# Expert product of a PEER layer: one 512-column matmul for both parts of the tokens under the high weight part

## The chip, the cores and the metric

The kernel runs on one core of a Trainium2 chip. The metric is the device time in microseconds (us) of one execution, the median over several runs. The engines of the core are named as in the profile: PE does matmuls (PEld is the loading of its stationary operand), DVE, ACT and POOL are the vector, scalar and general engines, SP issues transfers. Eight banks of accumulators in PSUM stand between PE and the engines that read its results; everything else lies in SBUF.

## The reference

256 tokens of width 2048 pass through a gMLP block, a stick-breaking attention block, a block that mixes a short convolution with an mLSTM, and a PEER layer. Only the last one matters here:

```python
def peer_ffn(h, wq, keys, u, v):      # 8 heads, 16384 experts, top 16 per head and token
    q = (xt @ wq).reshape(-1, PEER_HEADS, 2, PEER_HALF)
    s = jnp.einsum('thpc,hpnc->thpn', q, keys)
    sv, si = lax.top_k(s, PEER_TOPK)                 # 16 best of 128 keys, twice per head
    ...                                              # 16 best of the 256 pairs: eid, softmax gate
    ue = jnp.take(u, eid, axis=0)
    act = jax.nn.gelu(jnp.einsum('thkd,td->thk', ue, xt), approximate=False)
    ve = jnp.take(v, eid, axis=0)
    return jnp.einsum('thk,thkd->td', gate * act, ve)
```

## The kernel before

**No gathering.** The kernel multiplies all 16384 rows of `u` with all tokens, applies Gelu, multiplies with a dense 16384 x 256 gate matrix that is zero but for the chosen experts, and multiplies the result with all of `v`. So the PEER layer is two large products: the first expert product over `in_pu` (the table `u`, stage A below) and the second over `in_pv` (accumulator `y`).

**Two parts of a number.** Matmuls take fp32r operands. To keep fp32 accuracy each operand is split into a high part (rounded to fp32r) and a low part (the rest), and a product is three matmuls: high x high, low weight x high token, high weight x low token. For the weights the class `Stream` (L87) does the split as the tables arrive: SP loads a raw tile of 128x2048 (1 MB, three buffers), ACT copies each half of it to `wh` (L123, shown as L194, since ACT's operations all go through one helper; six buffers), DVE subtracts to get `wl` (L131, five buffers). Both buffers are reused when PE has finished the half that held them. `ahead` (L139) issues these steps as far ahead as the buffers reach, so that in DVE's queue the subtraction for a half stands four halves ahead of that half's matmuls. For the tokens the split is done once, in `affine_prep` (L784), into two tiles `nh` (high) and `nl` (low).

**The first expert product** (loop L1269 over `u` in 0..31, 512 experts each) calls `gemm_t` (L381) once per `u`. Its table tile holds, per raw tile, 4 slices of 128 of the contraction (2048 = 16 slices) for all 512 experts. One half of a raw tile is 2 slices x 4 blocks of 128 experts. The experts' block is the stationary operand, the 256 tokens are the moving one. Each of the 8 (slice, block) cells of a half takes three matmuls of 256 columns, L395 (high x high), L397 (high weight, low token), L398 (low weight, high token), all added in PSUM in the same 256 columns: 24 matmuls per half, 192 per `u`. The 512 experts x 256 tokens fill two banks (`acc0`, `acc1`, two buffers each). After the last half of a `u`, ACT applies Gelu to the two banks (the lines `f<-acc`, 128x512) and SP stores the 512 KB result to DRAM (`Ad`, L1275), from where the second product loads it again.

**Background work.** Generators registered in `bg` are advanced by one yield at each `bg.step()`; `gemm_t` steps once after each half. During stage A the background holds `route` (L1143): for each of four groups of two heads (three of them in stage A, the first one mostly before it) and each of two token halves it does the key scores on PE (L411, L1156) and the two top-16 searches and the gate on DVE (L1131 to L1199), with an Exp on ACT. `scatter` (L1205) then queues the gates on POOL, one indirect transfer for each column. When nearly all `u` are done, `first_v` loads the first two stored activations and the gates, and `prep_v` (L1241) multiplies them and splits the result for the second product, one line per step.

**What sets the order.** Nothing is scheduled: each engine executes its instructions in the order in which the Python code emits them, and waits at each for the semaphores of what it needs.

Of the kernel before, what the change touches and what calls it, by code (L numbers as in the profile page):

```python
# [5 lines left out]
F32 = mybir.dt.float32  # L6
# [5 lines left out]
P = 128  # L12
D = 2048
T = 256
# [155 lines left out]
def _block(ctx, tc, A, out):  # L170
# [153 lines left out]
    def tokens(x, kk, t):  # L324

        if isinstance(x, list):
            return x[0][:, kk // 2, (2 * t + kk % 2) * P:(2 * t + kk % 2 + 1) * P]
        return x[:, kk, t * P:(t + 1) * P]
# [52 lines left out]
    def gemm_t(xh, xl, evac):  # L381


        acc = [pp.tile([P, 512], F32, name=nm("acc"), tag=f"acc{b}", bufs=2) for b in range(2)]
        for kp in range(NKT // 2):
            if kp:
                bg.step()
            wh, wl = st.next()
            for k in range(2):
                kk = kp * 2 + k  # L390
                xa, xb = (x[0][:, kp].rearrange("p (h k c) -> p k c h", h=2, k=2)[:, k] for x in (xh, xl))
                for b in range(4):
                    o = acc[b // 2][:, (b % 2) * T:(b % 2 + 1) * T].rearrange("p (c h) -> p c h", h=2)
                    c = k * 512 + b * P
                    E.matmul(o, wh[:, c:c + P], xa, start=kk == 0 and b % 2 == 0, stop=False,  # L395
                             skip_group_check=True)
                    E.matmul(o, wh[:, c:c + P], xb, start=False, stop=False, skip_group_check=True)  # L397
                    E.matmul(o, wl[:, c:c + P], xa, start=False, stop=kk == NKT - 1,  # L398
                             skip_group_check=True)
        evac(acc)  # L400
        bg.step()
# [382 lines left out]
    def affine_prep(c, d, gname, bname, paired=False):  # L784
# [3 lines left out]
        nl = tile("xs", [NKT // 2, 2 * T], F32R, bufs=4)  # L788
        if not paired:
            nh, nl = (x.rearrange("p a (k t) -> p (a k) t", k=2) for x in (nh, nl))  # L790
# [7 lines left out]
        def go(n):  # L798
            for pr in range(2):
# [18 lines left out]
                if paired:  # L818
                    hv, lv = (x[:, k // 2].rearrange("p (h k c) -> p k h c", h=2, k=2) for x in (nh, nl))
# [20 lines left out]
        return ([nh], [nl], need) if paired else (nh, nl, need)  # L840
# [279 lines left out]
    x3h, x3l, prep3 = affine_prep(*ln_scales(st6), "l1g", "l1b", True)  # L1120
# [148 lines left out]
    for u in range(NU):  # L1269
        def ev(acc, u=u):  # L1270
            a = ft(1, [2, 512])
            for b in range(2):
                act(a[:, b].rearrange("p (e h c) -> p e c h", e=2, h=2),
# [134 lines left out]
```

## Time and profile before

| | us |
|---|---|
| median of 3 runs | 3069.61 |
| lowest and highest of the 3 | 3068.31, 3072.02 |
| the profiled execution, its own time | 3071.64 |
| its span, first to last instruction | 3069.9 |

Start, end and duration of each instruction come from the profiled execution alone. Its own time is 1.7 us longer than its span. Stage A, the first expert product, goes from 1689 to 2389 us of the span, the second product from there to the end. A duration of a matmul in the trace (275 ns for 256 columns) is the time from its start to its modelled end; matmuls overlap, so what one costs is the distance from its start to the next one's start.

### The profile page before, as it was taken

How to read it: one execution, taken by the hardware profiler on the slowest of the kernel's cores; microseconds unless marked ns; L12 is line 12 of the kernel's file. 1: busy time of each engine (PE TensorE's matmuls, PEld its weight loads, DVE VectorE, ACT ScalarE, POOL GpSimd, SP SyncE). 2: the span in 40 equal slices, each digit the busy share in tenths (PEclk: the TensorE clock that was granted, in tenths of full speed). 3: DMA queues.
4: the chain of work that ended last, by engine and by line, in shares of the span. 5: the costliest groups of instructions: out<-in, count | busy, mean ns of one | idle time of the engine just before them, and what ended most of it. 6: DMA issues, size and time to landing. Idle time of an engine off the chain costs nothing.

```text
span 3069.9 us, 42972 instructions
## 1 busy us (share of the span) xinstructions
PE 3022.8 (98%) x17276; PEld 2732.7 (89%) x17276; DVE 1914.0 (62%) x2486; ACT 1502.5 (49%) x1638; POOL 553.1 (18%) x275
## 2 busy tenths in 40 slices
PE   8999999999999999999999999999999999999997
PEld 7888888888888887888888999999999888888886
DVE  6565556666555566656558989644445666666666
ACT  5454445444554555544444555544445444444443
POOL 0000000000000000000001668888883000000001
PEclk9999999999999999999999999999999999999999
DMA  7776666666555565556656777777777987888874
GB/s 275 248 248 215 218 221 224 219 213 220 197 188 200 197 233 195 206 202 208 229 187 203 208 214 210 229 222 216 227 217 262 319 274 274 283 283 285 279 256 151
DMA packets 230616, 702.55 MB, mean 229 GB/s; under 512 B 50577, under 2 KB 144913, under 8 KB 158865
## 3 DMA queue, kind: packets, MB, share of 16 engines
q1 hardware_dynamic: 192912, 697.57, 66.2%
q0 software_dynamic: 37504, 2.25, 2.8%
q8 instruction: 135, 2.21, 0.3%
q14 instruction: 65, 0.52, 0.0%
HBM read 647.18 MB, written 52.56 MB: 228 GB/s over the span
## 4 chain that ended last, share of the span: by engine, by line
PE 95%; DVE 3%; ACT 1%; DMA 1%; issue 0%; SPq 0%; DVEq 0%; ACTq 0%
PE acc L343 16%; PE acc L344 16%; PE acc L345 16%; PE acc L398 7%; PE acc L397 7%; PE acc L395 7%; PE y L345 7%; PE y L343 7%; PE y L344 7%; DVE wl L131 1%; PE ms L411 1%; PE ms L565 0%; ACT xs L194 0%; DVE res L1293 0%; PE ms L692 0%
## 5 line engine op out<-in xcount | busy, mean ns | idle before, releaser
L131 DVE TENSOR_TENSOR wl<-raw,wh 128x1024 fp32r<-128x1024 f32 x1106 | 1343.1, 1222 | 825.8 <-PE acc L344 308.9
L194 ACT ACTIVATE wh<-raw 128x1024 fp32r<-128x1024 f32 x1106 | 1166.0, 1058 | 1259.2 <-PE acc L345 578.6
L1210 POOL DMA_INDIRECT Gd<-f x256 | 536.7, 2096 | 1790.2 <-DVE f L1199 1670.1
L343 PE MATMUL acc<-wh,xs 128*128 128x512 f32 x2112 | 813.1, 385 | 14.6 <-ACT wh L194 10.1
L344 PE MATMUL acc<-wl,xs 128*128 128x512 f32 x2112 | 803.5, 380 | 0.5 <-DVE wl L131 0.5
L345 PE MATMUL acc<-wh,xs 128*128 128x512 f32 x2112 | 803.2, 380 | 0.0
L398 PE MATMUL acc<-xs,wl 128*128 128x256 f32 x2048 | 564.1, 275 | 1.6 <-DVE wl L131 1.6
L395 PE MATMUL acc<-xs,wh 128*128 128x256 f32 x2048 | 564.7, 276 | 0.0
L397 PE MATMUL acc<-xs,wh 128*128 128x256 f32 x2048 | 563.9, 275 | 0.0
L343 PEld LDWEIGHTS acc<-wh,xs 128*128 128x128 f32 x2112 | 400.9, 190 | 73.6 <-ACT wh L194 10.1
L345 PEld LDWEIGHTS acc<-wh,xs 128*128 128x128 f32 x2112 | 400.7, 190 | 57.5 <-DVE xs L824 0.5
L344 PEld LDWEIGHTS acc<-wl,xs 128*128 128x128 f32 x2112 | 401.1, 190 | 56.3 <-DVE wl L131 1.0
L398 PEld LDWEIGHTS acc<-xs,wl 128*128 128x128 f32 x2048 | 393.9, 192 | 1.8 <-DVE wl L131 1.8
L395 PEld LDWEIGHTS acc<-xs,wh 128*128 128x128 f32 x2048 | 394.0, 192 | 0.0
L397 PEld LDWEIGHTS acc<-xs,wh 128*128 128x128 f32 x2048 | 394.0, 192 | 0.0
L343 PE MATMUL y<-wh,xs 128*128 128x512 f32 x1024 | 388.1, 379 | 0.0
L344 PE MATMUL y<-wl,xs 128*128 128x512 f32 x1024 | 388.1, 379 | 0.0
L345 PE MATMUL y<-wh,xs 128*128 128x512 f32 x1024 | 388.1, 379 | 0.0
L345 PEld LDWEIGHTS y<-wh,xs 128*128 128x128 f32 x1024 | 193.5, 189 | 27.5
L344 PEld LDWEIGHTS y<-wl,xs 128*128 128x128 f32 x1024 | 193.5, 189 | 27.5
L343 PEld LDWEIGHTS y<-wh,xs 128*128 128x128 f32 x1024 | 193.5, 189 | 27.4
L1296 POOL TENSOR_TENSOR res<-res,xs 128x512 f32<-128x512 f32 x6 | 9.7, 1643 | 718.7 <-DVE res L1293 718.7
(220 smaller groups left out, 1778.5 us busy)
## 6 DMA issues: line engine op xcount, KB each, us to landing
raw<-in_pu_dram SPq DMA_DIRECT2D x128, 1024.0 KB, 4.9
raw<-in_pv_dram SPq DMA_DIRECT2D x128, 1024.0 KB, 5.2
raw<-in_bwi_dram SPq DMA_DIRECT2D x64, 1024.0 KB, 4.9
raw<-in_w_dram SPq DMA_DIRECT2D x56, 1024.0 KB, 5.5
Gd<-zero SPq DMA_DIRECT2D x64, 512.0 KB, 7.0
raw<-in_aw_u_dram SPq DMA_DIRECT2D x32, 1024.0 KB, 5.8
raw<-in_aw_z_dram SPq DMA_DIRECT2D x32, 1024.0 KB, 6.0
raw<-in_awo_dram SPq DMA_DIRECT2D x32, 1024.0 KB, 5.8
```

What stands on the lines that cost most here:

```text
L131: self.nc.vector.tensor_tensor(l, raw[:, j * 1024:(j + 1) * 1024], self.hi[q].bitcast(F32), op=ALU.subtract)
L194: S.activation(out, in_, func, **kw)
L343: E.matmul(o, a, wa, start=first and opens, stop=False)
L344: E.matmul(o, a, wb, start=False, stop=False)
L345: E.matmul(o, b, wa, start=False, stop=fin and closes)
L395: E.matmul(o, wh[:, c:c + P], xa, start=kk == 0 and b % 2 == 0, stop=False, skip_group_check=True)
L397: E.matmul(o, wh[:, c:c + P], xb, start=False, stop=False, skip_group_check=True)
L398: E.matmul(o, wl[:, c:c + P], xa, start=False, stop=kk == NKT - 1, skip_group_check=True)
L411: E.transpose(p[:, jj * T + t * P:jj * T + (t + 1) * P], src(t, pr * 2 + jj), ident)
L1210: nc.gpsimd.indirect_dma_start(out=Gd[t][hh].rearrange("e c -> (e c)")[:, None], out_offset=bass.IndirectOffsetOnAxis(ap=idx[:, t, at:at + ...
L1296: (nc.gpsimd if t == 0 or n in (1, 2) else V).tensor_tensor(v, v, gb[1][:, (n - 1) * 512:n * 512], op=ALU.add)
```

## The change

**The table** is laid out anew on the host: a raw tile now holds all 16 slices of the contraction for one block of 128 experts, so that its two halves are slices 0 to 7 and 8 to 15 of that block. **The tokens** lie anew too: the two SBUF tiles are still two, but the first now holds the high and the low parts of slices 0 to 7 side by side, the second those of slices 8 to 15. **gemm_t** is called once per block (four times per `u`) and per slice issues two matmuls: the high weight with 512 columns, which are the 256 high and the 256 low token parts, into a whole bank (L391), and the low weight with the 256 high parts into that bank's first half (L393). The bank's two halves are then two partial sums of the same 128 x 256 result. **The evacuation** adds them on DVE with a tensor_reduce from PSUM to SBUF (L1273), once per block; ACT applies Gelu to two blocks at a time, from SBUF in place, and the store follows after the fourth block. The loop's bank alternates between `acc0` and `acc1`. The number of steps per `u` is still eight; `done_u` is now marked after the last step of a `u` and not before it.

```diff
--- before.py
+++ after.py
@@ -323,9 +323,7 @@
 
     def tokens(x, kk, t):
 
-        if isinstance(x, list):
-            return x[0][:, kk // 2, (2 * t + kk % 2) * P:(2 * t + kk % 2 + 1) * P]
-        return x[:, kk, t * P:(t + 1) * P]
+        return x(kk, t) if callable(x) else x[:, kk, t * P:(t + 1) * P]
 
     def gemm(xh, xl, kmap, evac, need={}, by_token=False, acc=None, opens=True, closes=True):
 
@@ -378,25 +376,22 @@
         bg.step()
         return r
 
-    def gemm_t(xh, xl, evac):
-
-
-        acc = [pp.tile([P, 512], F32, name=nm("acc"), tag=f"acc{b}", bufs=2) for b in range(2)]
-        for kp in range(NKT // 2):
-            if kp:
+    def gemm_t(x, evac):
+
+
+        acc = pp.tile([P, 512], F32, name=nm("acc"), tag=f"acc{rot('acct', (0, 1))}", bufs=2)
+        lo = acc[:, 0:T].rearrange("p (c h) -> p c h", h=2)
+        both = acc.rearrange("p (a c h) -> p a c h", a=2, h=2)
+        for half in range(2):
+            if half:
                 bg.step()
             wh, wl = st.next()
-            for k in range(2):
-                kk = kp * 2 + k
-                xa, xb = (x[0][:, kp].rearrange("p (h k c) -> p k c h", h=2, k=2)[:, k] for x in (xh, xl))
-                for b in range(4):
-                    o = acc[b // 2][:, (b % 2) * T:(b % 2 + 1) * T].rearrange("p (c h) -> p c h", h=2)
-                    c = k * 512 + b * P
-                    E.matmul(o, wh[:, c:c + P], xa, start=kk == 0 and b % 2 == 0, stop=False,
-                             skip_group_check=True)
-                    E.matmul(o, wh[:, c:c + P], xb, start=False, stop=False, skip_group_check=True)
-                    E.matmul(o, wl[:, c:c + P], xa, start=False, stop=kk == NKT - 1,
-                             skip_group_check=True)
+            for k in range(8):
+                m = x[half][:, k].rearrange("p (h a c) -> p a c h", h=2, a=2)
+                E.matmul(both, wh[:, k * P:(k + 1) * P], m, start=half == 0 and k == 0, stop=False,
+                         skip_group_check=True)
+                E.matmul(lo, wl[:, k * P:(k + 1) * P], m[:, 0], start=False, stop=half == 1 and k == 7,
+                         skip_group_check=True)
         evac(acc)
         bg.step()
 
@@ -786,6 +781,7 @@
 
         nh = tile("xs", [NKT // 2, 2 * T], F32R, bufs=4)
         nl = tile("xs", [NKT // 2, 2 * T], F32R, bufs=4)
+        both = (nh, nl)
         if not paired:
             nh, nl = (x.rearrange("p a (k t) -> p (a k) t", k=2) for x in (nh, nl))
 
@@ -816,7 +812,8 @@
                             scale=PVC(gname, k), bias=PVC(bname, k))
                 k = 4 * n + 2 * pr
                 if paired:
-                    hv, lv = (x[:, k // 2].rearrange("p (h k c) -> p k h c", h=2, k=2) for x in (nh, nl))
+                    v = both[k // 8][:, k % 8:k % 8 + 2].rearrange("p k (h a c) -> p a k h c", h=2, a=2)
+                    hv, lv = v[:, 0], v[:, 1]
                     tv = tmp.rearrange("p k (h c) -> p k h c", h=2)
                 else:
                     hv, lv, tv = nh[:, k:k + 2], nl[:, k:k + 2], tmp
@@ -837,7 +834,10 @@
         for n in range(1, 4):
             task = bg.add(later(n, task))
             need[n] = [task]
-        return ([nh], [nl], need) if paired else (nh, nl, need)
+        if paired:
+            part = lambda a: lambda kk, t: both[kk // 8][:, kk % 8, (2 * t + a) * P:(2 * t + a + 1) * P]
+            return part(0), part(1), need, both
+        return nh, nl, need
 
     def residual_affine(gname, bname, alloc):
 
@@ -1117,7 +1117,7 @@
 
     rgb = tile("xs", [4, 1024], bufs=4)
     q7t = tile("xs", [4, 1024], bufs=4)
-    x3h, x3l, prep3 = affine_prep(*ln_scales(st6), "l1g", "l1b", True)
+    x3h, x3l, prep3, x3 = affine_prep(*ln_scales(st6), "l1g", "l1b", True)
 
 
     keysT = tile("phaseA", [16, P])
@@ -1267,14 +1267,16 @@
     done_u = set()
     fv = bg.add(first_v())
     for u in range(NU):
-        def ev(acc, u=u):
-            a = ft(1, [2, 512])
-            for b in range(2):
-                act(a[:, b].rearrange("p (e h c) -> p e c h", e=2, h=2),
-                    acc[b].rearrange("p (e c h) -> p e c h", e=2, h=2), AF.Gelu)
-            nc.sync.dma_start(out=Ad[u], in_=a.rearrange("p b (e t) -> p (b e) t", e=2))
-            done_u.add(u)
-        gemm_t(x3h, x3l, ev)
+        a = ft(1, [4, T])
+        for b in range(4):
+            def ev(acc, b=b):
+                V.tensor_reduce(a[:, b].rearrange("p (h c) -> p c h", h=2),
+                                acc.rearrange("p (a c h) -> p c h a", a=2, h=2), axis=mybir.AxisListType.X, op=ALU.add)
+                if b % 2:
+                    act(a[:, b - 1:b + 1], a[:, b - 1:b + 1], AF.Gelu)
+            gemm_t(x3, ev)
+        nc.sync.dma_start(out=Ad[u], in_=a)
+        done_u.add(u)
     bg.finish(fv)
     bg.drain()
 
@@ -1373,7 +1375,7 @@
          "bwi": _gemm_tiles(f["b_w_in"][0]), "bwo": _gemm_tiles(f["b_w_out"][0]),
          "w2": _gemm_tiles(w2[:, :7168]), "w2g": _gate_rows(w2[:, 7168:].T).reshape(P, NKT, P).transpose(2, 1, 0).reshape(P, 2048),
          "wo2": _gemm_tiles(f["w_out_2"][0]), "wq": _gemm_tiles(f["peer_wq_2"][0]),
-         "pu": _by_second_key(f["peer_u_2"][0]).reshape(NU, 512, 4, 4, P).transpose(0, 2, 4, 3, 1).reshape(NU, 4, P, 2048),
+         "pu": _by_second_key(f["peer_u_2"][0]).reshape(NU, 4, P, NKT, P).transpose(0, 1, 4, 3, 2).reshape(NU, 4, P, 2048),
          "pv": _by_second_key(f["peer_v_2"][0]).reshape(NU, 4, P, 4, 256, 2).transpose(0, 3, 2, 1, 5, 4).reshape(NU, 4, P, 2048)}
     cw = f["conv_w_2"][0]
     pvec = {"g0": _kt(f["norm_g"][0]), "g1": _kt(f["norm_g"][1]), "lig": _kt(f["ln_in_g_2"]),
```

**On PE**, one half of a weight tile in the middle of stage A. Before, the second and the third of its eight cells, three matmuls each (`xs_603` holds the high token parts, `xs_604` the low ones):

```order
L395 MATMUL acc_739_15690<-xs_603_11831,wh675_15554 128x256
L397 MATMUL acc_739_15690<-xs_604_11832,wh675_15554 128x256
L398 MATMUL acc_739_15690<-xs_603_11831,wl675_15588 128x256
L395 MATMUL acc_740_15691<-xs_603_11831,wh675_15554 128x256
L397 MATMUL acc_740_15691<-xs_604_11832,wh675_15554 128x256
L398 MATMUL acc_740_15691<-xs_603_11831,wl675_15588 128x256
```

In the changed kernel, from the last slices of one half (`wh674`) to the first of the next (`wh675`), two matmuls each (`xs_603` now holds both parts of slices 0 to 7, `xs_604` of 8 to 15):

```order
L393 MATMUL acc_760_15111<-xs_603_11831,wl674_15007 128x256
L391 MATMUL acc_760_15111<-xs_603_11831,wh674_14975 128x512
L393 MATMUL acc_760_15111<-xs_603_11831,wl674_15007 128x256
L391 MATMUL acc_760_15111<-xs_604_11832,wh675_15005 128x512 [waits Activation_49]
L393 MATMUL acc_760_15111<-xs_604_11832,wl675_15031 128x256 [waits DVE_49]
```

A half goes from 24 matmuls of 256 columns to 8 of 512 and 8 of 256: the same 6144 columns, with 16 loads of the stationary operand where there were 24.

**On DVE**, in the stretch where a top-16 search runs in the background (the MAX, MAX_INDEX and MATCH_REPLACE rows, on scores in `e0`), from one low half of the stream to the second after it. Before:

```order
L131 TENSOR_TENSOR wl606_13011<-raw303_12797,wh606_12969 128x1024 [waits DMAHW5_49,PE_49,Activation_49]
L1134 MAX f3_659_12964<-e0_658_12934 128x8 [waits DVE_49]
L1135 MAX_INDEX f3_659_12964<-f3_659_12964,e0_658_12934 128x8 [waits DVE_49]
L1131 MAX f3_659_12964<-e0_658_12934 128x8
L1132 MAX_INDEX f3_659_12964<-f3_659_12964,e0_658_12934 128x8 [waits DVE_49]
L131 TENSOR_TENSOR wl607_13043<-raw303_12797,wh607_13009 128x1024 [waits PE_49,Activation_49]
L1133 MATCH_REPLACE e0_658_12934<-f3_659_12964,e0_658_12934 128x128 [waits DVE_49]
L1134 MAX f3_659_12964<-e0_658_12934 128x8 [waits DVE_49]
L1135 MAX_INDEX f3_659_12964<-f3_659_12964,e0_658_12934 128x8 [waits DVE_49]
L1131 MAX f3_659_12964<-e0_658_12934 128x8
L131 TENSOR_TENSOR wl608_13077<-raw304_12903,wh608_13041 128x1024 [waits DMAHW6_49,PE_49,Activation_49]
```

In the changed kernel:

```order
L131 TENSOR_TENSOR wl606_12953<-raw303_12775,wh606_12920 128x1024 [waits DMAHW5_49,Activation_49]
L1134 MAX f3_662_12915<-e0_660_12892 128x8 [waits DVE_49]
L1135 MAX_INDEX f3_662_12915<-f3_662_12915,e0_660_12892 128x8 [waits DVE_49]
L1131 MAX f3_662_12915<-e0_660_12892 128x8
L1132 MAX_INDEX f3_662_12915<-f3_662_12915,e0_660_12892 128x8 [waits DVE_49]
L131 TENSOR_TENSOR wl607_12977<-raw303_12775,wh607_12951 128x1024 [waits PE_49,Activation_49]
L1273 TENSOR_REDUCE f1_663_12949<-acc_664_12950 128x128x2 [waits DMAHW0_49,PE_49]
L1133 MATCH_REPLACE e0_660_12892<-f3_662_12915,e0_660_12892 128x128 [waits DVE_49]
L1134 MAX f3_662_12915<-e0_660_12892 128x8 [waits DVE_49]
L1135 MAX_INDEX f3_662_12915<-f3_662_12915,e0_660_12892 128x8 [waits DVE_49]
L1131 MAX f3_662_12915<-e0_660_12892 128x8
L131 TENSOR_TENSOR wl608_13005<-raw304_12868,wh608_12975 128x1024 [waits DMAHW6_49,Activation_49]
```

A tensor_reduce of 128x512 inputs to 128x256 stands behind every second subtraction. It waits for PE to have finished the block (four halves back in the stream), and this one, the first of its `u`, also for a transfer: it writes the buffer `f1` from which the store of the `u` before is read.

**On ACT**, around one Gelu late in stage A. Before, both banks at the end of a `u`, read from PSUM and written with stride (128x2x128x2):

```order
L194 ACTIVATE wh698_16365<-raw349_16247 128x1024 [waits DMAHW6_49,DVE_49,PE_49]
L194 ACTIVATE wh699_16395<-raw349_16247 128x1024 [waits DVE_49,PE_49]
L194 ACTIVATE wh700_16423<-raw350_16311 128x1024 [waits DMAHW0_49,DVE_49,PE_49]
L194 ACTIVATE wh701_16453<-raw350_16311 128x1024 [waits DVE_49,PE_49]
L194 ACTIVATE wh702_16481<-raw351_16369 128x1024 [waits DMAHW1_49,DVE_49,PE_49]
L194 ACTIVATE f1_753_16511<-acc_751_16277 128x2x128x2 [waits DMAHW7_49,PE_49]
L194 ACTIVATE f1_753_16511<-acc_752_16278 128x2x128x2 [waits PE_49]
L194 ACTIVATE wh703_16517<-raw351_16369 128x1024 [waits DVE_49]
```

In the changed kernel:

```order
L194 ACTIVATE wh698_15647<-raw349_15560 128x1024 [waits DMAHW6_49,PE_49,Activation_49]
L194 ACTIVATE f1_775_15581<-f1_775_15581 128x512 [waits DMAHW7_49,DVE_49,Activation_49]
L194 ACTIVATE wh699_15672<-raw349_15560 128x1024 [waits PE_49]
L194 ACTIVATE wh700_15692<-raw350_15607 128x1024 [waits DMAHW0_49,PE_49]
L194 ACTIVATE wh701_15716<-raw350_15607 128x1024 [waits PE_49,Activation_49]
L194 ACTIVATE wh702_15736<-raw351_15651 128x1024 [waits DMAHW1_49,PE_49,Activation_49]
L194 ACTIVATE f1_775_15581<-f1_775_15581 128x512 [waits DVE_49]
L194 ACTIVATE wh703_15763<-raw351_15651 128x1024 [waits PE_49,Activation_49]
```

The two Gelus of a `u` stand four halves apart, read SBUF, and wait for DVE where they waited for PE.

## Rows read from the trace of the kernel before

**Rows 1.** The profile's page: busy share of each engine, and the longest chain by engine.
```profile
PE 3022.8 (98%) x17276; PEld 2732.7 (89%) x17276; DVE 1914.0 (62%) x2486; ACT 1502.5 (49%) x1638; POOL 553.1 (18%) x275
...
PE 95%; DVE 3%; ACT 1%; DMA 1%; issue 0%; SPq 0%; DVEq 0%; ACTq 0%
```

**Rows 2.** Busy time by stretch: search stretch, rest of stage A, its head, clock dip.
```profile
core 0: us, PE busy (x) PEld busy (x) DVE busy (x) ACT busy (x) POOL busy (x), PEclk, DMA share, GB/s
1715.86:1949.88 234.02, 234.02 (x2099) 234.02 (x2097) 209.51 (x541) 131.35 (x135) 174.11 (x97) 1.00 0.74 216
1949.88:2367.90 418.02, 418.02 (x3746) 418.02 (x3745) 192.26 (x157) 201.60 (x195) 340.65 (x152) 1.00 0.75 230
1688.05:1715.86 27.81, 23.73 (x190) 23.21 (x189) 26.25 (x61) 10.46 (x14) 18.20 (x12) 0.94 0.65 180
1710.50:1716.00 5.50, 5.48 (x34) 5.48 (x35) 4.70 (x9) 3.78 (x5) 3.23 (x3) 0.69 0.95 270
```

**Rows 3.** Waits in 1715.86 to 1949.88: us in total, times, longest.
```profile
DVE wl L131 <- ACT wh L194: 7.3, 4, 3.9
DVE wl L131 <- PE acc L398: 5.9, 10, 1.4
...
DVE wl L131 <- PE acc L397: 0.7, 1, 0.7
```

**Rows 4.** Timeline of PE: in stage A, and in the second product (28 matmuls apart).
```profile
1944.52 0.28 PE L395 MATMUL acc<-xs,wh 128*128 128x256 f32 x1
...
2449.83 0.38 PE L344 MATMUL y<-wl,xs 128*128 128x512 f32 x1
...
2455.88 0.38 PE L345 MATMUL y<-wh,xs 128*128 128x512 f32 x1
```

**Rows 5.** Longest chain, 1700 to 1960: start, us, what (128 columns each).
```profile
1748.19 0.89 PE ms L1156 x8
```

**Rows 6.** Timeline of DVE: whole-row operations that follow each other.
```profile
1677.02 0.68 DVE L853 TENSOR_TENSOR res<-res,xs 128x512 f32<-128x512 f32 x1
1677.74 0.69 DVE L854 TENSOR_TENSOR res<-res,xs 128x512 f32<-128x512 f32 x1
1678.35 1.22 DVE L131 TENSOR_TENSOR wl<-raw,wh 128x1024 fp32r<-128x1024 f32 x1
```

**Rows 7.** Groups of DVE by form: busy us, mean ns, idle before.
```profile
L1187 DVE TENSOR_REDUCE f<-e 128x16 f32<-128x256 f32 x32 | 13.4, 420 | 1.1
...
L1080 DVE COPY f<-acc 128x512 f32<-128x512 f32 x4 | 2.8, 691 | 1.7 <-PE acc L345 1.7
```

**Rows 8.** Groups of ACT by form in 1715.86 to 1949.88.
```profile
L194 ACT ACTIVATE f<-acc 128x512 f32<-128x512 f32 x22 | 22.5, 1132 | 4.3 <-PE acc L398 4.2
...
L194 ACT ACTIVATE e<-ms 128x512 f32<-128x512 f32 x5 | 2.9, 587 | 2.5 <-PE ms L1156 2.5
```

**Rows 9.** Timeline of DVE at the search stretch's end.
```profile
1938.56 1.22 DVE L131 TENSOR_TENSOR wl<-raw,wh 128x1024 fp32r<-128x1024 f32 x1
...
1941.45 1.23 DVE L131 TENSOR_TENSOR wl<-raw,wh 128x1024 fp32r<-128x1024 f32 x1
```

**Rows 10.** Waits of PE in 1688.05 to 1715.86, the head of stage A.
```profile
PE ms L1156 <- ACT f L194: 2.5, 1, 2.5
PE acc L398 <- DVE wl L131: 1.6, 1, 1.6
```

**Rows 11.** Transfers of tile Ad from 1700 to 1960.
```profile
DMA to landing us min/median/max: 2.6/3.3/7.7
```

**Rows 12.** Timelines at stage A's end: POOL's last loads, ACT, DVE, and PE's first `y`.
```profile
2332.18 3.71 POOL L1237 DMA_DIRECT2D f<-Gd  x5 [0.69 <-DMA Gd<-f]
...
2366.68 1.22 DVE L1247 TENSOR_TENSOR f<-f,f 128x1024 f32<-128x1024 f32 x1
...
2386.18 1.22 DVE L1253 TENSOR_TENSOR xs<-f,xs 128x1024 fp32r<-128x1024 f32 x1 [0.66 <-ACT xs L194]
...
2389.40 0.38 PE L343 MATMUL y<-wh,xs 128*128 128x512 f32 x1
```

## The prediction

> **What bounds the kernel now.** I read the page first: PE is busy 98% of the span and carries 95% of the longest chain, DVE is busy 62% and ACT 49% [rows 1]. Means hide stages, so the second view is busy time by stretch [rows 2]. From 1949.88 to 2367.90 us, most of stage A, PE has no gap and DVE is busy 192.26 of 418.02 us (46%): PE alone sets the time. From 1715.86 to 1949.88, while the top-16 searches run, PE has no gap either, but DVE is busy 209.51 of 234.02 us (90%). The third view, the waits of that stretch, says how much of the rest is room: DVE waited for PE to free a low buffer for only 5.9 + 0.7 = 6.6 us, and for ACT's high halves 7.3 us [rows 3]; the other 10 us are small gaps between operations that depend on each other. So stage A has two parts, one with a free DVE and one in which DVE just keeps up. The change takes work from PE and gives work to DVE, so the two parts will answer differently.
>
> **PE: eight pairs for eight triples.** In the free part 3746 matmuls start or reach into 418.02 us, two of them over its edges [rows 2]: 418.02 / 3744 = 111.7 ns each, 335.0 ns for three, 2.68 us for a half of 24. In the second product 28 starts of 512 columns take 2455.88 - 2449.83 = 6.05 us [rows 4]: 216.1 ns each. Two times 111.7 is 223.3, so a 512-column matmul is 7.2 ns cheaper than two of 256. The pair 512 + 256 has no row. If the 256 keeps its slot, the pair takes 216.1 + 111.7 = 327.8 ns and saves 7.2. If the 256 falls to half of the 512's slot, 108.0 ns, the pair saves 10.9. If the new token pattern costs back what fusing saves, it saves nothing. I take 7.2: eight score matmuls of only 128 columns take 0.89 us in the chain, also 111 ns each [rows 5], which looks like a floor under each matmul (a weight load, say) rather than a price of columns; they are plain fp32, so this is a hint only. A half then takes 2.62 us, 58 ns less.
>
> [...]
>
> From 1949.88 to 2389.40, where the first `y` starts, lie 439.5 / 2.68 = 164 halves: **-9.5 us** (bounds 0 and -14.3).
>
> **DVE: 128 reductions.** No row shows a reduction from 512 to 256. DVE's cost is by what it reads: a reduction of 256 inputs takes 420 ns, a copy of 512 from PSUM 691 ns [rows 7]. An independent operation starts before the one ahead has ended: 1678.35 - 1677.74 = 0.61 us behind one of 0.69 [rows 6]. I take 0.61 us, since the next row in DVE's queue seldom needs the sum. Below: 0.45, a little over what the 256-input reduction would hold DVE (0.42 less the same 0.08 is 0.34). Above: 0.85, for the strided writing; a Gelu of 512 that writes with stride takes 1132 ns against 587 for a plain copy of that size [rows 8], though Gelu and stride can't be told apart there.
>
> [...]
>
> In the free part a reduction adds 0.3 us to the 1.2 that DVE does per half of 2.62: hidden. **In the search stretch** it is not. There are 234.02 us and 85 halves, so 42.5 reductions, 25.9 us. Against that stand the 6.6 us that DVE waited for PE, and the lead: DVE works ahead, and PE stalls when the lead is gone. It is shortest at the end of the searches, where a low half is ready at 1938.56 + 1.22 = 1939.78 and its matmuls start at 1944.52 [rows 4, 9] (paired by counting both back from the stage's end, 165 halves before the last): 4.7 us. The waits for ACT come where ACT itself waited for DVE's gate and then had to load tables and do two Gelus; with one shorter Gelu there I count half of the 7.3 us as regained, 3.6. So PE finishes the stretch 25.9 - 6.6 - 4.7 - 3.6 = **11.0 us later** (bounds 0.5, all of ACT's waits regained and 0.45 per reduction, and 24.8, none and 0.85). PE's own gain of 85 x 0.058 us is not collected here: DVE sets the pace. Afterwards DVE needs 1.5 us per half and rebuilds its lead, but the time stays lost. PE will stand for 2 us and more at the long search steps, and the clock may fall: in 1710.50 to 1716.00, just after PE had waited 2.5 us, the granted clock was 0.69, worth 0.31 x 5.5 = 1.7 us [rows 2, 10]. While DVE sets the pace such a dip only uses up standing time.
>
> **The head of stage A**, to 1715.86: DVE is busy 26.25 of 27.81 us [rows 2] and PE waits for it, directly or through ACT [rows 10]. Two reductions stand there: **+1.2 us**.
>
> **The store.** The first reduction of each `u` waits until the store of the last one has been read out of `f1`. From the end of the last reduction: Gelu 0.6 to 1.0 us, issue 0.3, landing 3.3 [rows 8, 11], so 4.2 to 4.6. Between the two reductions DVE has two halves' work, (234.02 - 6.6 - 7.3) / 85 = 2.59 each, 5.2 us: mostly no wait, but where two short steps fall together it stands 1 to 2 us. Eleven `u` lie in the stretch: **+1.5 us** (bounds 0 and 11). In the free part DVE's lead covers it.
>
> **Edits at nothing.** Gelu moves from PSUM to SBUF: ACT is half idle. The token parts are written by the same operations to other places. The first gates arrive on POOL's queue, last issue 2332.18 + 3.71, and are first used at 2366.68 [rows 12]; a stage 10 us shorter still finds them there. `prep_v` comes one step later: its last split, at 2386.18 before [rows 12], would end some 5 us after the first `y` starts, when half of the first pair's work, 24 matmuls of 216 ns, 5.2 us, is done: just hidden, at most 2.6 us if not. The second product itself does not change.
>
> **Sum.** -9.5 + 11.0 + 1.2 + 1.5 = +4.2 us on the profiled execution's 3071.64 (its span and 1.7 around it). That execution stands 2.0 above the median of the three, so 3069.61 + 4.2 = 3073.8: no change that can be told. About 0.2% (6.1 us) is what a measurement here can tell from none.
>
> **Rivals.**
> - *DVE keeps up, faster.* The reduction holds DVE 0.45 us, ACT's waits vanish, the pair saves 10.9 ns: -14.3 + 0.5 + 0.9 = -12.9, 3056.7. For it: the 256-input reduction. Against: the copy of 512 from PSUM.
> - *The 256 shrinks beside a 512.* [...] For it: two lengths give two prices per column. Against: the 128-column row.
> - *The reduction is dear, slower.* Its strided write makes it 0.85 us: 44.5 x 0.24 = 10.7 more, 3084.5. It decides from 0.65 us on. For it: the strided Gelu. Against: rows 7.
> - *The store stands in DVE's way, slower.* Landing takes 1 us longer and each of eleven `u` waits: +8, 3082.
> - *PE gains nothing.* The pair takes 335 ns: 3083.3. Then the change does only its harm.
>
> **From cases to numbers.** The forecast has 0.38, the rivals in their order 0.15, 0.14, 0.20, 0.08, 0.05. Faster by over 0.2% is the first rival and a little of the forecast's spread, 0.17; slower is the last three and a twelfth of the forecast, 0.36; within 0.2% the rest, 0.47. The likeliest alone runs from 3068 to 3080. The range 3061 to 3085 takes in the dear reduction and stops short of the first rival's end.
>
> **What would show it.** Right: in the free part a half takes 2.62 us with 16 matmuls and PE still has no gap; in the search stretch PE now waits at L393 for DVE's `wl`, some 15 to 20 us in sum, and DVE's waits for PE fall to about none; the reduction (L1273) shows near 690 ns. Wrong: no wait of PE there; a reduction well off 690 ns; a wait for the store's landing at the first reduction of most `u`; PE waiting at the first `y`.

## The result, and the profile after

| | changed kernel | before, beside it |
|---|---|---|
| median of 4 runs each, us | 3087.6 (3086.17 to 3088.77) | 3068.96 (3068.01 to 3072.02) |
| ratio | 1.0055, 95% interval 1.0043 to 1.0068 | |
| profiled execution, us | 3088.12 | 3071.64 |

The changed kernel is slower by 18.6 us. Forecast were 4.2, with a range up to 3085.0. The page of the changed kernel, busy time and the longest chain by engine:

```profile
PE 3016.9 (98%) x15228; PEld 2669.0 (86%) x15228; DVE 1987.1 (64%) x2614; ACT 1472.7 (48%) x1638; POOL 472.2 (15%) x275
...
PE 87%; DVE 9%; DMA 2%; ACT 1%; issue 1%; SPq 0%; DVEq 0%; ACTq 0%
```

PE is even 5.9 us less busy than in [rows 1], yet carries 87% of the chain where it carried 95%; DVE has 9% of it for 3%, transfers 2% for 1%. The busy time by stretch tells where (columns as in [rows 2]). The first row is the search stretch (the same halves as the first of [rows 2]), the second the free part up to 2385.40, the last four are the stretches in which the granted clock was 0.50:

```profile
1717.10:1975.44 258.34, 238.13 (x1418) 216.87 (x1417) 229.15 (x580) 115.73 (x132) 192.20 (x107) 0.96 0.69 188
1975.44:2385.40 409.96, 409.11 (x2499) 375.98 (x2498) 240.39 (x238) 187.12 (x197) 239.03 (x139) 1.00 0.77 237
1709.46:1716.29 6.83, 5.41 (x19) 4.95 (x20) 5.02 (x10) 5.17 (x8) 4.85 (x4) 0.50 0.76 217
1794.79:1801.62 6.83, 5.41 (x19) 4.95 (x20) 3.54 (x4) 5.17 (x8) 4.01 (x3) 0.50 0.94 278
1869.89:1873.30 3.41, 3.41 (x11) 2.96 (x12) 3.31 (x9) 2.85 (x4) 2.94 (x2) 0.50 0.91 202
1883.54:1893.78 10.24, 5.47 (x19) 4.95 (x20) 7.78 (x17) 7.38 (x10) 8.72 (x6) 0.50 0.60 145
```

The search stretch grew from 234.02 to 258.34 us, and PE, which had no gap there, stands for 20.2 of them. In the free part 2499 matmuls take 409.96 us, 164.0 ns each, 328.1 a pair; that holds 0.85 us in which PE stands at its start, and behind it, where PE has no gap, a half takes 2.62 us and a pair 327.5 ns. Waits from 1686 to 2010 us, which takes in the head and the tail of the searches (us in total, times, longest):

```profile
ACT f L194 <- DVE f L1194: 44.4, 7, 11.7
...
PE ms L1156 <- ACT f L194: 19.1, 3, 8.0
DVE f L1273 <- DMA Ad<-f: 18.5, 7, 4.3
...
PE acc L393 <- DVE wl L131: 8.9, 8, 2.5
...
DVE f L1273 <- PE acc L393: 7.0, 5, 2.4
...
DVE wl L131 <- PE acc L393: 1.6, 2, 0.8
```

PE stands 28.0 us in all, 4.1 before [rows 10]. Two thirds are not a wait for `wl`: three times PE stops at the score matmuls (L1156), for a copy by ACT. And DVE stands 18.5 us for the store of `f1`. One such place on four engines, in order of time for each (start, duration, what, idle before it):

```profile
1869.84 0.33 SPq L108 DMA_DIRECT2D raw<-in_pu_dram  x1
1871.10 0.33 SPq L1278 DMA_DIRECT2D Ad<-f  x1
...
1869.73 0.69 DVE L1273 TENSOR_REDUCE f<-acc 128x256 f32<-128x512 f32 x1
...
1877.87 0.69 DVE L1273 TENSOR_REDUCE f<-acc 128x256 f32<-128x512 f32 x1 [3.02 <-DMA Ad<-f]
...
1883.86 0.19 DVE L1194 TENSOR_TENSOR f<-f 128x32 f32<-128x32 f32 x1
...
1884.08 0.23 ACT L194 ACTIVATE f<-f 128x32 f32<-128x32 f32 x1 [8.86 <-DVE f L1194]
...
1885.85 1.28 ACT L194 ACT_TABLE_LOAD   x1 [0.60 <-issue]
1887.14 0.63 ACT L194 ACTIVATE f<-f 128x512 f32<-128x512 f32 x1
1887.68 1.07 ACT L194 ACTIVATE f<-ms 128x512 f32<-128x512 f32 x2
...
1888.31 2.08 PE L1156 MATMUL ms<-phaseA,f 128*128 128x128 f32 x8 [8.01 <-ACT f L194]
...
1890.82 0.63 PE L391 MATMUL acc<-xs,wh 128*128 128x512 f32 x1
1891.25 0.42 PE L393 MATMUL acc<-xs,wl 128*128 128x256 f32 x1
1891.46 0.63 PE L391 MATMUL acc<-xs,wh 128*128 128x512 f32 x1
```

Read it from the top. The last reduction of a `u` ends at 1870.42, the store is issued 0.7 us later, 1.26 us behind a raw tile of 1 MB, and the next `u`'s first reduction stands 3.02 us until it has landed. DVE reaches the gate's subtraction (L1194) at 1883.86. ACT has stood 8.86 us for it with its Exp; behind the Exp come a table load, a Gelu and the two copies of the next route's queries, and only then PE's score matmuls can go: PE stood 8.01 us. When it starts again its clock is at half, and a pair takes 0.64 us (1890.82 to 1891.46).

The landing of the store, once in the search stretch (1717 to 1975) and once in the free part (2000 to 2380):

```profile
DMA to landing us min/median/max: 3.7/5.9/6.7
...
DMA to landing us min/median/max: 3.4/3.8/8.2
```

The second row also holds two loads of `f` from `Ad`, the 8.2 among them; the longest store there took 5.6 us.

### The profile page after: what moved, and what is told of

It reads as the page before. It is cut to its first block, busy times and chain, and to the rows that moved or that the text cites. A ratio compares the mean times of both kernels' runs of the same rounds, so it can differ in the third digit from the quotient of the medians.

```text
span 3086.3 us, 38962 instructions
## 1 busy us (share of the span) xinstructions
PE 3016.9 (98%) x15228; PEld 2669.0 (86%) x15228; DVE 1987.1 (64%) x2614; ACT 1472.7 (48%) x1638; POOL 472.2 (15%) x275
## 4 chain that ended last, share of the span: by engine, by line
PE 87%; DVE 9%; DMA 2%; ACT 1%; issue 1%; SPq 0%; DVEq 0%; ACTq 0%
PE acc L341 16%; PE acc L342 16%; PE acc L343 16%; PE acc L391 10%; PE y L343 7%; PE y L342 7%; PE y L341 7%; PE acc L393 5%; DVE wl L131 3%; DMA Ad<-f 1%; DVE f L1273 1%; PE ms L406 1%; DVE f L1135 0%; DVE e L1185 0%; PE ms L560 0%
## 5 line engine op out<-in xcount | busy, mean ns | idle before, releaser
L1210 POOL DMA_INDIRECT Gd<-f x256 | 455.9, 1781 | 1792.8 <-DVE f L1199 1668.0
L391 PE MATMUL acc<-xs,wh 128*128 128x512 f32 x2048 | 679.3, 385 | 0.0
L393 PE MATMUL acc<-xs,wl 128*128 128x256 f32 x2048 | 562.2, 275 | 8.9 <-DVE wl L131 8.9
L391 PEld LDWEIGHTS acc<-xs,wh 128*128 128x128 f32 x2048 | 390.5, 191 | 54.8
L393 PEld LDWEIGHTS acc<-xs,wl 128*128 128x128 f32 x2048 | 396.5, 194 | 11.6 <-DVE wl L131 11.5
L1273 DVE TENSOR_REDUCE f<-acc 128x256 f32<-128x512 f32 x128 | 88.5, 692 | 126.9 <-PE acc L393 95.2
L194 ACT ACTIVATE f<-f 128x512 f32<-128x512 f32 (+1 forms) x72 | 42.2, 586 | 232.1 <-DVE f L1273 180.6
```

Of the source, the lines that this page charges most:

```text
L194: S.activation(out, in_, func, **kw)
L391: E.matmul(both, wh[:, k * P:(k + 1) * P], m, start=half == 0 and k == 0, stop=False, skip_group_check=True)
L393: E.matmul(lo, wl[:, k * P:(k + 1) * P], m[:, 0], start=False, stop=half == 1 and k == 7, skip_group_check=True)
L1210: nc.gpsimd.indirect_dma_start(out=Gd[t][hh].rearrange("e c -> (e c)")[:, None], out_offset=bass.IndirectOffsetOnAxis(ap=idx[:, t, at:at + ...
L1273: V.tensor_reduce(a[:, b].rearrange("p (h c) -> p c h", h=2), acc.rearrange("p (a c h) -> p c h a", a=2, h=2), axis=mybir.AxisListType.X, ...
```

## The experiments

Thirteen kernels. Chips differ a little (medians of the kernel before on four of them: 3070.50, 3070.68, 3071.23 and 3071.80 us), so each is given by its difference to the kernel before run beside it on the same chip ("before" below); the changed kernel is at +18.6.

**Are the reductions the cause?** e2 leaves them out (the matmuls with the low token parts still run, but nothing reads their result), e4 adds as many to the kernel before, with their results unused.

```diff
-                V.tensor_reduce(a[:, b].rearrange("p (h c) -> p c h", h=2),
-                                acc.rearrange("p (a c h) -> p c h a", a=2, h=2), axis=mybir.AxisListType.X, op=ALU.add)
-                if b % 2:
-                    act(a[:, b - 1:b + 1], a[:, b - 1:b + 1], AF.Gelu)
+                act(a[:, b].rearrange("p (h c) -> p c h", h=2),
+                    acc[:, 0:T].rearrange("p (c h) -> p c h", h=2), AF.Gelu)
```

e2: 

> The changed kernel without the DVE addition: Gelu reads the product of the high token parts from PSUM, and the product with the low token part (columns 256 to 511 of the accumulator) is left out of the output; the matmuls, loads and stores are the same. Both the queue and the balance theory: with DVE's load as before the change, only TensorE's shorter halves are left, 9.5 us from the free part of the stretch and up to 5 us from the search: 3055 to 3062 us. If something else in the change costs (the layout of the table, the weight loads between matmuls, the head): 3069 us or more.

```diff
                 act(a[:, b].rearrange("p (e h c) -> p e c h", e=2, h=2),
                     acc[b].rearrange("p (e c h) -> p e c h", e=2, h=2), AF.Gelu)
+                for e in range(2):
+                    V.tensor_reduce(et(6, [T]).rearrange("p (h c) -> p c h", h=2),
+                                    acc[b].rearrange("p (a c h) -> p c h a", a=2, h=2), axis=mybir.AxisListType.X, op=ALU.add)
```

e4: 

> The kernel before with four extra DVE reductions of 512 columns (the form of the changed kernel's, 128 in all) behind each tile's Gelus, their results used by nothing; matmuls, table and Gelus as before. If the reductions' place in DVE's queue is the whole cost (queue or balance theory): the 28 us that the changed kernel loses in the search stretch, without the 9 us that its matmuls give back: 3090 to 3100 us. If DVE's time is nearly free and the loss comes from the new matmuls, the layout or the store: 3069 to 3077 us.

Measured: e2 **-13.4** (ratio 0.9957, 0.9942 to 0.9972), e4 **+25.7** (1.0085, 1.0070 to 1.0101). Without the reductions the change gains. The reductions alone, on the old matmuls, cost more than the whole change lost. But e4's are not the changed kernel's: each stands behind the Gelu of its bank, and DVE waits 17.7 us for it. The waits from 1686 to 2010, first of e4, then of e2:

```profile
DVE e L1276 <- ACT f L194: 17.7, 9, 2.5
...
PE ms L1156 <- ACT f L194: 11.6, 3, 5.7
...
PE acc L398 <- DVE wl L131: 9.9, 8, 2.7
```

```profile
PE ms L1156 <- ACT f L194: 4.5, 1, 4.5
```

e2 shows one loss that isn't the reductions': its first stop at L1156, at the head of stage A, lasts 4.5 us, 2.5 before [rows 10]. From half 1 to half 8 e2 falls 3.1 us behind the kernel before, and the changed kernel 3.4.

**The store.** e3 gives the table products a second buffer, e8 stores each half of the one buffer by itself.

```diff
-        a = ft(1, [4, T])
+        a = ft(0 if u % 2 and u < 28 else 1, [4, T])
```

```diff
                 if b % 2:
                     act(a[:, b - 1:b + 1], a[:, b - 1:b + 1], AF.Gelu)
+                    nc.sync.dma_start(out=Ad[u][:, b - 1:b + 1], in_=a[:, b - 1:b + 1])
...
-        nc.sync.dma_start(out=Ad[u], in_=a)
```

e3: 

> The changed kernel with a second SBUF buffer for the table products, so that the first reduction of a tile never waits for the store of the tile before (31.7 us in 14 waits of DVE). Store theory: DVE gets these us back while it sorts, 3070 to 3078 us. Queue and balance theory: most of these waits lie in the free part, or where DVE would have waited for ScalarE anyway; 3 to 6 us come back, 3081 to 3085 us.

e8: 

> The changed kernel, but each half of the table products' buffer is stored as soon as its Gelu is issued: two transfers of 256 KB per tile instead of one of 512 KB, the first of them four halves earlier and the second before the step instead of after it. One buffer still. Store theory: the first reduction of a tile finds the first half stored long ago and the third one finds the second half stored, DVE's wait for Ad is near 0 and the time that of the kernel with two buffers, 3072 to 3076 us. If the second buffer helped by something else than this wait: 3080 us or more.

Measured: e3 **+2.8** (1.0010, 1.0001 to 1.0019), e8 **+11.1** (1.0036, 1.0022 to 1.0050). The store is worth 15.8 us. I had expected 3 to 6 in e3 from the queue theory, and that was wrong. e8 keeps part of the wait, where near 0 was expected; the waits from 1686 to 2010, first of e8, then of e3, which has none for `Ad`:

```profile
PE ms L1156 <- ACT f L194: 19.1, 3, 8.1
DVE f L1273 <- DMA Ad<-f: 11.6, 7, 3.4
...
PE acc L393 <- DVE wl L131: 5.2, 3, 2.3
```

```profile
PE ms L1156 <- ACT f L194: 14.6, 3, 5.3
...
PE acc L393 <- DVE wl L131: 3.5, 2, 1.9
```

With DVE standing 18.5, 11.6 and 0 us for the store the kernel loses 18.6, 11.1 and 2.8: above e3, 0.7 to 0.9 us for each.

**Queue order or DVE's time?** After the result my first theory was that PE's stops at L1156 are the loss: an Exp that waits for DVE holds up ACT's copies for PE. The rival was that DVE simply has too much to do while it searches. e1 puts the Exp four halves later; e5 does so with the second buffer, e7 in the kernel before.

```diff
+            for _ in range(4):
+                yield
             act(ex, ex, AF.Exp)
```

e1: 

> The changed kernel with one edit: in each route, four halves pass between the DVE subtraction (L1194) and the Exp on ScalarE that needs it, so that ScalarE reaches the Exp when DVE is already past the subtraction. Queue theory: most of the loss is not DVE's time but the order of the queues; PE's score matmuls (L1156) stand behind a ScalarE copy, which stands behind an Exp, which waits for DVE four halves behind. Then ScalarE's wait for the subtraction (44.4 us, 7 times) falls under 10 us, PE's wait at L1156 (19.1 us, 3 times) is gone, and the time is 3066 to 3075 us. Balance theory: DVE simply has about 26 us too much work while it sorts, so the same standing comes back as PE's waits for wl: 3083 to 3089 us. Store theory (DVE waits 31.7 us for the store of the table products to free their buffer): no change, 3085 to 3089 us.

e5: 

> The changed kernel with both edits, the second buffer for the table products and the Exp four halves later. Two costs that add (store wait 13.6 us, queue order 10.8 us, as their runs alone gave): 3087.6 - 13.6 - 10.8 = 3063 us, and neither DVE's wait for Ad nor PE's wait at L1156 is left. One cost with two handles (the store wait matters only where it stands ahead of the Exp's subtraction): no better than the better one alone, 3071 to 3075 us.

e7: 

> The kernel before with the Exp four halves later, nothing else. If the order of the queues costs only when DVE is behind, there is little to get here: the wait of PE at L1156 (2.5 us, once) and the clock fall behind it go, 3064 to 3068 us. If the late Exp is a gain of its own that has nothing to do with the change: 3058 us or less. If moving the next route by eight halves costs elsewhere: over 3070 us.

Measured: e1 **+5.6** (1.0018, 1.0009 to 1.0027), e5 **-22.4** (0.9929, 0.9915 to 0.9942), e7 **-6.1** (0.9980, 0.9971 to 0.9989). e1 came out between its theories (its waits at L1156 fell to 6.1 us, those for `wl` stayed at 9.2, and at 11.6 up to 2110, since its searches run on), and e5 15 us below its lower forecast. In e5 stage A has no gap and the clock does not fall:

```profile
1686.00:2400.00 714.00, 714.00 (x4334) 655.72 (x4333) 537.55 (x933) 345.45 (x374) 461.45 (x262) 1.00 0.80 234
```

But the late Exp also spreads the searches over eight more halves per route, so it gives DVE room too. e9 moves the Exp without spreading (a task of its own, while the route goes on); e10 spreads without moving it; both have two buffers (the first edit below is that of e9 and e11, the second that of e10 and e13). e11 is e4 with the Exp apart, e13 is e10 with one buffer.

```diff
-            act(ex, ex, AF.Exp)
...
+            gates.append(bg.add(gate(n, t, ex, es)))
+            yield
+
+    def gate(n, t, ex, es):
+        for _ in range(3):
+            yield
+        act(ex, ex, AF.Exp)
+        yield
+        V.tensor_reduce(es, ex, axis=mybir.AxisListType.X, op=ALU.add)
...
```

```diff
             V.tensor_copy(sif, si)
+            for _ in range(4):
+                yield
```

e9: 

> The changed kernel with the second buffer, and the Exp with the normalization behind it as a task of its own: it comes four halves after the subtraction, while the route goes on at once, so the searches stay as close together as in the changed kernel (the kernel with the late Exp spread them over eight more halves per route). Order theory: what mattered was only that ScalarE's copies for the score matmuls no longer stand behind an Exp that waits for DVE: 3048 to 3053 us, as with the late Exp, PE never waiting at L1156. Room theory: the late Exp helped because DVE got 8 more halves per route for the same searches and reductions; without them DVE falls behind and PE waits for wl: 3060 to 3072 us.

e10: 

> The changed kernel with the second buffer, the Exp directly behind its subtraction as in the changed kernel, and four halves without work put into the middle of each search (eight per route, as many as the late Exp adds). Room theory: DVE has the time it needs, 3048 to 3053 us. Order theory: the Exp still waits for DVE and the score matmuls behind it; with DVE four halves behind in its queue the wait at L1156 stays at 2 to 3 places, 3060 to 3072 us.

e11: 

> The kernel before with the 128 extra reductions (which alone cost 26 us) and the Exp as a task of its own, four halves late. Order theory: the reductions cost nothing as long as no queue couples DVE's backlog to the score matmuls: 3064 to 3070 us, as the kernel before with the late Exp and no reductions (3064.6). Room theory: most of the 26 us stay: 3080 to 3092 us.

Measured: e9 **+1.6** (1.0005, 0.9996 to 1.0014), e10 **-19.3** (0.9936, 0.9923 to 0.9950), e11 **+13.7** (1.0043, 1.0027 to 1.0058). Room does nearly all that the late Exp did, and the queue theory as I had put it falls. In e10 PE has no wait for `wl`, and this at L1156 (1686 to 2010):

```profile
PE ms L1156 <- ACT f L194: 2.7, 3, 1.0
```

e11 says that order has a part: 12.0 us less than e4; PE's 11.6 us at L1156 are 1.1 there, but its waits for `wl` have gone from 9.9 to 15.8. e9 didn't test it cleanly. Its PE still stands 13.7 us at L1156, since a Gelu that waits for the reduction has taken the Exp's place ahead of the copies:

```profile
1876.04 0.63 ACT L194 ACTIVATE f<-f 128x512 f32<-128x512 f32 x1 [5.50 <-DVE f L1278]
1876.58 1.07 ACT L194 ACTIVATE f<-ms 128x512 f32<-128x512 f32 x2
...
1877.21 2.02 PE L1156 MATMUL ms<-phaseA,f 128*128 128x128 f32 x8 [4.52 <-ACT f L194]
```

So e12 puts the Gelus (with the store behind) four halves later as well, for 26 of 32 `u`.

```diff
+    def finish_u(u, b, a):
+        for _ in range(4):
+            yield
+        act(a[:, b - 1:b + 1], a[:, b - 1:b + 1], AF.Gelu)
+        if b == 3:
+            nc.sync.dma_start(out=Ad[u], in_=a)
+            done_u.add(u)
...
                 if b % 2:
-                    act(a[:, b - 1:b + 1], a[:, b - 1:b + 1], AF.Gelu)
+                    g = finish_u(u, b, a)
+                    if u < 26:
+                        bg.add(g)
+                    else:
+                        bg.finish(bg.add(g))
```

e12: 

> The changed kernel with the second buffer, the Exp apart as in the run before, and each Gelu four halves after its reduction too (for the first 26 tiles), with the store behind it: nothing on ScalarE then waits for DVE's backlog, which the run with the Exp alone apart did not reach (there a Gelu that waited 5.5 us for the reduction took the Exp's place ahead of the copies). The searches stay as close together as in the changed kernel. Order theory: PE's waits at L1156 go and nothing takes their place, 3050 to 3060 us. Room theory: DVE has too much to do in these 95 halves, and the standing comes back as PE's waits for wl; what is gained is the clock falls and the too long stalls at most: 3062 to 3072 us.

e13: 

> The changed kernel with four halves without work in each search, as in the run with room, but with its one buffer for the table products. If the store wait costs only by taking time from a DVE that has none to spare, the room covers most of it: 3052 to 3060 us against 3052.5 with two buffers. If the wait costs by itself (reduction, Gelu, store and next reduction are one chain that can't be hurried, whatever room there is): 3066 to 3078 us, as with the late Exp and one buffer (3076.8 against 3048.3).

Measured: e12 **-6.5** (0.9977, 0.9968 to 0.9986), e13 **+6.4** (1.0019, 1.0010 to 1.0028). Stage A of e12 by busy time, and PE's one wait of note from 1686 to 2010:

```profile
1686.00:2400.00 714.00, 702.02 (x4263) 642.40 (x4262) 531.81 (x920) 337.00 (x366) 462.97 (x264) 1.00 0.79 229
```

```profile
PE acc L393 <- DVE wl L131: 12.0, 12, 2.3
```

Nothing stops at L1156, the clock stays at 1.00 in spite of twelve waits, and what is left is 12.0 us of waits for `wl`, with DVE busy 288.72 of the first 314.00 us. That is what e12's room theory said. Order, of Exp and Gelu together, is worth 9.3 us (e3 to e12), room about 15.9 (e12 to e5, where the Gelus also stand early again). Taken the other way round, room comes first with 22.1 us (e3 to e10) and the late Exp adds 3.1 (e10 to e5, whose intervals overlap): the two overlap, so neither has a price of its own. e13 came out where its second expectation put it: room does not pay for the store's wait. With room one buffer costs 25.7 us (e13 against e10), with the late Exp 28.0 (e1 against e5). Its waits from 1686 to 2010:

```profile
DVE f L1275 <- DMA Ad<-f: 21.7, 8, 4.1
...
PE ms L1156 <- ACT f L194: 16.6, 3, 7.2
```

The three stops come at the ends of routes: at halves 14, 50 and 86 of stage A a half takes 8.5, 9.9 and 11.7 us, in e10 4.6 to 4.8. Two halves before the second of these the half's `wl` was ready 0.6 us ahead of PE, and 5.1 us in e10. The store's waits eat the lead, and the queue then makes a long stop of a small shortage. So the two edits of e5 give 41.0 us together and 28.8 (13.0 and 15.8) one by one: with one buffer, the store's waits use up what room there is.

**A hybrid.** e6 keeps three matmuls of 256 columns and no reduction for the first 12 `u`, and the new form for the other 20.

```diff
+                    E.matmul(o, wh[:, w], m[:, 0], start=b == half == k == 0, stop=False, skip_group_check=True)
+                    E.matmul(o, wh[:, w], m[:, 1], start=False, stop=False, skip_group_check=True)
+                    E.matmul(o, wl[:, w], m[:, 0], start=False, stop=half == 1 and k == 7, skip_group_check=True)
...
-        for b in range(4):
+        for b in range(0 if u < 12 else 4):
```

e6: 

> The changed kernel, but for the first 12 of 32 tiles of the table (about the stretch in which DVE sorts) each block is multiplied in three matmuls of 256 columns into the same 256 columns, with Gelu from PSUM and no reduction; the pair of 512 and 256 with the reduction stands only in the other 20 tiles. Every theory in which the loss stands in the search stretch and comes from the reductions: the gain of the free part alone, 160 halves x 0.058 = 9.3 us, 3060 to 3063 us (DVE's wait for the store stays in the free part and costs nothing there). If part of the loss belongs to the new layout or order of the blocks: 3066 us or more.

Measured: **-6.2** (0.9980, 0.9971 to 0.9989); a little short of the 9.3 us, which its interval (-8.9 to -3.4) just misses. The trace has the missing 3 us at the head, before any reduction: from half 1 to half 8 e6 falls 3.4 us behind the kernel before, with a stop of 4.8 us at its score matmuls (2.5 before) and 6.8 us at the half clock (3.4 before). It then keeps pace through the searches and gains 9.5 us behind them. Why the head loses this with the new layout, in e2 and e6 as in the changed kernel, stays open. The fastest kernel is e5: 3048.3 us, 22.4 below the kernel before, of which the late Exp alone gave 6.1. The pairs' 14.9 us (256 halves by 0.058) and the 4.1 us of standing and 1.7 of clock that the kernel before loses make 20.7 of the 22.4.

## Why the prediction was wrong

**The pair.** Right: 327.5 ns, forecast as 327.8, and a half 2.62 us; the rivals' 324.1 (216.1 + 108.0) and 335 are out. From half 97 to half 252, behind PE's last stand, its lag behind the kernel before fell from 26.4 to 17.1 us, 0.060 a half for 0.058 forecast.

**The reduction.** Right. By form, in stage A (mean ns, idle before):

```profile
L1273 DVE TENSOR_REDUCE f<-acc 128x256 f32<-128x512 f32 x126 | 87.2, 692 | 126.9 <-PE acc L393 95.2 <-DMA Ad<-f 31.7
```

691 was the row it was taken from [rows 7]; the trace says 692. The rival of a dear reduction is out.

**The store: the step that failed.** The forecast said "from the end of the last reduction: Gelu 0.6 to 1.0 us, issue 0.3, landing 3.3", so "mostly no wait", +1.5 us with 11 as the bound. Gelu and issue were even shorter (0.69 us from the reduction's end to the issue). The landing was taken as the median of [rows 11], whose longest, 7.7, stands beside it. The changed kernel's median in the searches is 5.9, so the buffer comes free 6.6 us after the reduction's end, and the forecast gave DVE 5.2 us of other work in that time. This is not by chance. DVE's last subtraction from a raw tile frees that buffer and so starts a load of 1 MB (it ended at 1869.81, the load was issued at 1869.84); the reduction is the next in DVE's queue, so when DVE is behind, the store mostly follows about 1.3 us after a load. Of the stores of the first twelve `u`, seven stand 1.26 to 1.28 us behind one and took 5.8 to 6.7; in the free part, where PE sets the time of the reduction, they stand 2.69 us behind, with a median of 3.8. The trace of before had the sign: its three stores issued 0.38 us behind a load took 7.0 to 7.7 us, and its others from 1700 to 1960, 2.8 to 3.7 us behind, 2.6 to 4.9. I take it from these landings that the load just ahead holds the store up; why it does was not shown, and no run here tries another queue. The rival "the store stands in DVE's way" had the right mechanism, landing over 1 us longer, at +8 and a chance of 0.08; measured are 15.8 us (e3). In the free part, as forecast, DVE's lead covers the wait: DVE stands 13.2 us for stores from 2000 to 2380, and PE not at all.

**What a wait of DVE costs.** The forecast priced a shortage of DVE one to one. Here it is dearer. Had PE gone on with 0.9 us of score matmuls at its three stops, it would have missed the next half's `wl` by 0.4, 1.2 and 2.7 us (an estimate from when each `wl` was ready: 1707.09, 1792.42 and 1883.94); in ACT's queue it stood 5.1, 5.9 and 8.0. And "such a dip only uses up standing time" is wrong: during the stop DVE regains its lead (in the second half behind the third stop `wl` is ready 9.6 us ahead of PE), so PE could run, and runs at a granted clock of 0.50. The four falls hold 68 matmuls, at most 34 pairs; each takes 0.64 for 0.33 us, 10.5 us at most, where the kernel before lost 1.7 [rows 2]. The account of the whole: 23.9 us more standing (28.0 - 4.1), up to 8.8 more at the half clock, 14.9 less for 256 halves by 0.058: +17.8; the profiled executions differ by 16.5.

**Search stretch and head.** By stretch (first low-weight matmul of halves 1, 8, 93 and 256), the changed kernel starts stage A 2.1 us earlier than the kernel before, loses 3.4 in the head (1.2 forecast) and 24.3 in the search stretch (11.0 and the store's 1.5), and gains 8.7 in the rest (9.5). In e3 the search stretch takes 245.21 us, 11.2 more than before, so 13.1 of the 24.3 are the store's, and that term alone takes the time out of the range. The head was mis-sized by 2.2 us, and its cause was wrong: e2 and e6, with no reduction there, lose 3.1 and 3.4. With the store out of the way, e3 measures +2.8 where the forecast without its store term says +2.7 (-9.5 + 11.0 + 1.2). The number is partly luck: e3 has 14.0 us more standing than before and half-clock stretches of 17.1 us against 3.4, and PE's own gain of some 5 us in the searches, which the forecast left out, sets off most of the clock's loss. That DVE is short of time there is shown by e10 and e5: given eight more halves per route and two buffers, it does all the reductions, and PE waits 2.7 us in e10 and not at all in e5.

**Edits at nothing.** One was not nothing. Gelu was left out since "ACT is half idle", but it now waits for DVE (90.0 us, 19 times, from 1686 to 2010), and it waits ahead of ACT's copies for PE: e12, with the Gelus and the stores behind them later too, is 8.1 us below e9.

**What would show it** was half right: PE's waits for `wl` were to be 15 to 20 us and are 8.9, with 19.1 more at L1156. DVE's waits for PE were to fall to about none: with its subtractions it waits 1.6 us, but 7.0 more with its reductions, some of it just behind PE's stops. And "a wait for the store's landing at the first reduction of most `u`" was named as the sign of being wrong, and it is there.

## What to carry to other kernels

Work given to an engine that just keeps up must be priced with every wait that it brings to that engine; a wait on a single buffer is its transfer's landing time at the place where it will be issued, with what the same engine starts just ahead of it, and not the median of a quieter stretch (here 5.9 us and not 3.3). When a late engine stands in front of another engine's in-order queue, look what else is in that queue: shortages of an estimated 0.4 to 2.7 us became stops of 5 to 8. And before a change that loads an engine is thrown away, look whether that engine's background work can be spread: the change cost 18.6 us with one buffer and crowded searches, and gained 22.4 with two buffers and eight more halves per route (with the late Exp, which alone gave 6.1).

## What the runs showed of the hardware that was not expected

- While the searches ran, a 512 KB store issued 1.26 to 1.28 us behind a 1 MB load on the same queue landed after 5.8 to 6.7 us; in the free part, 2.69 us behind one, after a median of 3.8 (3.4 to 5.6).
- With PE's stands of 5.1, 5.9, 2.5 and 8.0 us its granted clock fell to 0.50 for 6.8, 6.8, 3.4 and 10.2 us, and a pair of 512 and 256 columns took 0.64 us for 0.33. In e12 twelve waits, the longest 2.3 us, left it at 1.00; in e1 one of 2.4 us came with 3.4 us at 0.50.
- Each of the six Exps in the search stretch of the changed kernel came between two table loads of 1.28 us on ACT, one ahead of it and one ahead of the next Gelu, and at the stop shown above the second of them (1885.85) stood in the way of PE's score matmuls.
